# Feed-forward operands computed beside the second half of a mixer's out product, in pools of their own

## The chip, the cores and the metric

One core of a Trainium2 chip runs the whole program. The metric is the device time of one execution in microseconds (us), the median of several runs.

## The reference, cut to what matters

Two blocks on 512 tokens of 1024 features, in float32. The first (attention, neighbourhood attention, pooling, a long convolution, experts) isn't touched. The second puts 16 meta tokens ahead and runs two layers, each a mixer and then a SwiGLU:

```python
def _swiglu(h, w_gu, w_down):
    gate, up = jnp.split(h @ w_gu, 2, axis=-1)
    return (jax.nn.silu(gate) * up) @ w_down
...
    for layer in range(DEPTH_2):
        j = layer // 2
        if layer % 2 == 0:
            h = h + _mixer_rglru_swa(_rmsnorm(h, mix_norm_ab[j]), ...)
        else:
            h = h + _mixer_retention(_rmsnorm(h, mix_norm_ret[j]), ...)
        h = h + _swiglu(_rmsnorm(h, ffn_norm[layer]), ffn_w_gu[layer], ffn_w_down[layer])
```

Both mixers end in a product with an out matrix that is added to `h`: `concatenate([y_rnn, y_att]) @ w_out` and `(silu(g) * o) @ w_out`.

## The kernel before, in words

The residual `hT` holds the features on the partitions in 8 tiles f of 128 and the 528 tokens along a row. Every float32 product is three matmuls: `split` (L296, L299) makes a high part by a cast (ACT) and a low part by a subtraction (DVE), of weights and of activations, and PE adds high·high, high·low and low·high. Weights come over SP's DMA queue into a ring of three raw tiles with three split pairs `whi`, `wlo`.

**Mixer 0** (`mixer_ab`): RG-LRU and sliding-window attention write their outputs, split, to `abm0` and `abm1`. The out product (L2460 to L2464) runs over two halves o of the mix, and in each over eight rows f in the order `FORDER` = 0, 4, 1, 5, 2, 6, 3, 7: load and split one 128x512 weight tile, 24 matmuls (L1798: two token halves, four slices, three parts), and two adds to `hT` (L2464, DVE). **Mixer 1** (`mixer_ret`) does the same for two halves hh of its heads from `ry0`, `ry1`: 24 matmuls of 512 columns a row, one add (L2595).

**Feed-forward** (`swiglu`). The gate and up products use a Strassen-like scheme over four row pairs (f, f+4). For a row, ACT writes `hid0` = gain·hT (L2143), squares hT (L2145, L2148) and POOL sums the squares (L2149). When both rows of a pair are there, `operands` (L1826) makes seven parts of them: two subtractions on POOL (L1835, L1839), two on DVE (L1837, L1840), and splits of 264, 528 and 1056 columns into `xo0` and `xo1` (L296 on ACT, L299 on DVE). The four-part sums lie in a tile `s24` (pairs 0 and 2) or `rawF` (pairs 1 and 3). Both tiles also serve the weights: `rawF` is the fourth raw tile, `s24` holds sums of weight tiles.

A job is one of 22 row blocks of w_gu. Its weights are a plain tile (L1866, SP), a tile of sums, which is a plain load (L1871, SP) and then a second load that adds onto it from POOL's queue (L1876), and a half tile `a22` (L1981). ACT casts them (L1900, L1918, L1926, L1988), DVE or POOL makes the low parts (L1890, L1991), and PE runs four products A, Bb, C, D (L1852). Within the first job PE also does the sum for the norm (L2157), ACT and DVE make the scale R (L2158, L2159), and ACT copies a product for the gate (L2085, L2088, L2099). The down jobs follow each group (L2062, adds L2072). Weight pairs rotate over five slots: the ring's three, then F0, F1 of the feed-forward's pool.

What orders the work: each engine runs its instructions in order. PE's order is written by hand; those of ACT, DVE and POOL are set by a scheduler up to the first job and by hand from the second. Memory of a closed pool is handed on: the first write into a tile waits for the last use of what lay there. `swiglu` opened one pool after the mixer's pools had closed, with `hid0`, `xo0`, `xo1`, `rawF`, `s24` and the rest in it.

Of the kernel before, what the change touches and what calls it, by code (L numbers as in the profile page):

```python
# [2117 lines left out]

def swiglu(B, layer, cuts):
    b, nc, tc = B.b, B.nc, B.tc  # L2120
    V, S_, G, T_ = nc.vector, nc.scalar, nc.gpsimd, nc.tensor
    A = b.A
    o0, W = cuts[0][0], cuts[0][1] - cuts[0][0]
    gain = b.smv("ffng", 8 * layer, 8)
    with ExitStack() as es:
        pool = es.enter_context(tc.tile_pool(name=f"ffn{layer}", bufs=1, reuse_waits="tile"))
        es.enter_context(tc.manual_schedule(engines={mybir.EngineType.PE}))
        xo = [b.t(pool, [P, 4, 7 * W], F32R, tag="xo0")]
        b.t(pool, [P, 1056], tag="s24")
        b.t(pool, [P, 8, 2 * W], tag="hid1")  # L2130
        for i in range(FSLOTS):
            for n in ("whi", "wlo"):
                b.t(pool, [P, 1024], F32R, tag=f"{n}F{i}")
        b.t(pool, [P, 1, W], tag="p1")
        xo.append(b.t(pool, [P, 4, 7 * W], F32R, tag="xo1"))
        wn = Wino(B, pool, W, cuts, [(B.ring, "")] * 3 + [(pool, f"F{i}") for i in range(FSLOTS)],
                  [(B.ring, "raw")] * 3 + [(pool, "rawF")], b.hT)
        xg = b.t(pool, [P, 8, 2 * W], tag="hid0")
        R, a = b.t(B.xp, [P, 2 * W], tag="xR"), B.tmp(1)[:, :2 * W]
# [293 lines left out]

def mixer_ab(B, dbg):
    b, nc, tc = B.b, B.nc, B.tc
    A = b.A
    lin = B.cyc(0, 1, 2, 3, 6, 7)
    with ExitStack() as es:
# [20 lines left out]
        for o in range(2):
            for i, f in enumerate(FORDER):  # L2460
                acc = abo[0] if o == 0 and i < 4 else abo[1]
                w = load_split(b, B.ring, A["ab_out"][f, :, 512 * o:512 * o + 512], 512)
                for a, (a0, a1) in zip(B.lin(w, [m[:, 4 * o:4 * o + 4] for m in mix], HV, 4, acc=acc), HV):
                    nc.vector.tensor_tensor(b.hT[:, f, a0:a1], b.hT[:, f, a0:a1], a[:, :a1 - a0], op=ALU.add)  # L2464

# [3 lines left out]

def mixer_ret(B, dbg):  # L2470
    b, nc, tc = B.b, B.nc, B.tc
# [3 lines left out]
    with ExitStack() as es:  # L2475
        B.xx = es.enter_context(tc.tile_pool(name="xret", bufs=1, reuse_waits="tile"))
        pool = es.enter_context(tc.tile_pool(name="ret", bufs=1, reuse_waits="tile"))
        for i in range(2):
            b.t(pool, [P, 8, 512], tag=f"ry{i}")
# [121 lines left out]
def block2(b, out, dbg):  # L2601
    nc, tc = b.nc, b.tc
    with tc.tile_pool(name="hres", bufs=1, reuse_waits="tile") as hp, \
# [6 lines left out]

        def dump(n):
            if dbg is not None and n in dbg:
                nc.sync.dma_start(dbg[n].rearrange("(f p) n -> p f n", p=P), b.hT)
        mixer_ab(B, dbg)
        dump("h_ab")
        swiglu(B, 0, HV)
        dump("h_f0")
        mixer_ret(B, dbg)
        dump("h_ret")
        swiglu(B, 1, ((16, 272), (272, 528)))  # L2620
# [40 lines left out]
```

## Time and profile before

| | |
|---|---|
| median of 3 runs (lowest, highest) | 2386.99 us (2381.87, 2392.85) |
| the profiled execution: its own time | 2384.32 us |
| its span, mean granted TensorE clock | 2382.5 us, 0.957 |
| PE busy | 2204.3 us, 93% of the span |
| DVE, ACT, POOL busy | 1544.1, 1108.2, 823.9 us |

Times in views are microseconds from the start of the span. The 1.8 us between the span and the execution's own time lie outside the profile. An engine's idle time stands in brackets behind the instruction that ended it, with what released it.

### The profile page before, as it was taken

How to read it: one execution, taken by the hardware profiler on the slowest of the kernel's cores; microseconds unless marked ns; L12 is line 12 of the kernel's file. 1: busy time of each engine (PE TensorE's matmuls, PEld its weight loads, DVE VectorE, ACT ScalarE, POOL GpSimd, SP SyncE). 2: the span in 40 equal slices, each digit the busy share in tenths (PEclk: the TensorE clock that was granted, in tenths of full speed). 3: DMA queues.
4: the chain of work that ended last, by engine and by line, in shares of the span. 5: the costliest groups of instructions: out<-in, count | busy, mean ns of one | idle time of the engine just before them, and what ended most of it. 6: DMA issues, size and time to landing. Idle time of an engine off the chain costs nothing.

```text
span 2382.5 us, 34349 instructions
## 1 busy us (share of the span) xinstructions
PE 2204.3 (93%) x13248; PEld 1882.8 (79%) x13248; DVE 1544.1 (65%) x2138; ACT 1108.2 (47%) x1697; POOL 823.9 (35%) x543
## 2 busy tenths in 40 slices
PE   7799989978999888899699999999999997999999
PEld 1577768757777667767699999978788875999999
DVE  5764886557885776765687685665544555776854
ACT  4324654326876764545454353433323344543532
POOL 2325122225774644430344251322201213442512
PEclk9999989988999999979899999999999998899999
DMA  7563121577988752100365464422222222664652
GB/s 252 188 216 126 37 96 35 215 259 245 344 304 317 264 197 79 56 18 14 97 164 169 120 180 111 110 77 75 68 90 77 80 71 73 175 173 124 178 124 85
DMA packets 112289, 338.58 MB, mean 142 GB/s; under 512 B 14280, under 2 KB 17624, under 8 KB 112118
## 3 DMA queue, kind: packets, MB, share of 16 engines
q1 hardware_dynamic: 91168, 288.85, 35.6%
q0 software_dynamic: 11536, 31.75, 7.0%
q10 hardware_dynamic: 9414, 15.72, 2.0%
q8 instruction: 106, 1.74, 0.3%
q14 instruction: 65, 0.53, 0.1%
HBM read 325.65 MB, written 19.47 MB: 145 GB/s over the span
## 4 chain that ended last, share of the span: by engine, by line
PE 54%; DVE 4%; ACT 1%; issue 1%; POOL 1%; DMA 1%; DVEq 0%; POOLq 0%; ACTq 0%
PE p L1852 18%; PE p L1798 13%; PE p L2062 11%; PE p L2535 4%; PE p L2569 1%; PE p L2399 1%; DMA rawF<-in_gu 1%; PE p L1787 1%; PE p L2425 1%; PE p L2566 1%; PE p L2538 1%; DVE xo L299 0%; PE gu L1637 0%; PE p L2227 0%; PE p L2422 0%
## 5 line engine op out<-in xcount | busy, mean ns | idle before, releaser
L296 ACT CAST whi<-raw 128x1024 fp32r<-128x1024 f32 (+1 forms) x237 | 239.8, 1022 | 298.5 <-PE p L1798 132.6
L299 DVE TENSOR_TENSOR wlo<-raw,whi 128x1024 fp32r<-128x1024 f32 (+1 forms) x178 | 253.4, 1442 | 90.9 <-ACT whi L296 87.3
L1852 PE MATMUL p<-xo,whi 128*128 128x264 f32 (+1 forms) x1312 | 251.7, 291 | 42.4 <-DVE xo L299 15.1
L1852 PEld LDWEIGHTS p<-xo,whi 128*128 128x128 f32 x1312 | 209.2, 194 | 47.0 <-DVE xo L299 17.3
L1798 PE MATMUL p<-x,whi 128*128 128x264 f32 (+1 forms) x992 | 224.7, 330 | 4.4 <-DVE xt L2291 2.1
L299 POOL TENSOR_TENSOR wlo<-raw,whi 128x1024 fp32r<-128x1024 f32 x59 | 153.7, 2613 | 198.2 <-ACT whi L296 179.2
L1852 PE MATMUL p<-xo,wlo 128*128 128x264 f32 (+1 forms) x656 | 189.1, 288 | 3.3 <-DVE wlo L1890 3.3
L1798 PEld LDWEIGHTS p<-x,whi 128*128 128x128 f32 x992 | 157.7, 188 | 27.5 <-issue 5.2
L1852 PE MATMUL p<-xo,whiF 128*128 128x264 f32 (+1 forms) x800 | 149.1, 285 | 0.0
L1798 PE MATMUL p<-x,wlo 128*128 128x264 f32 (+1 forms) x496 | 141.2, 332 | 0.9 <-POOL wlo L299 0.9
L1852 PEld LDWEIGHTS p<-xo,wlo 128*128 128x128 f32 x656 | 127.4, 194 | 3.9 <-DVE wlo L1890 3.9
L1852 PEld LDWEIGHTS p<-xo,whiF 128*128 128x128 f32 x800 | 125.5, 191 | 0.0
L2062 PE MATMUL p<-hid,whi 128*128 128x264 f32 (+1 forms) x768 | 123.4, 282 | 0.0
L1360 PE MATMUL gu<-wlo,xh 128*128 128x512 f32 x272 | 110.6, 406 | 11.4 <-DVE wlo L299 6.2
L2072 DVE TENSOR_TENSOR hT<-hT,p 128x264 f32<-128x264 f32 (+1 forms) x96 | 36.5, 421 | 129.2 <-PE p L2062 129.2
L1852 PE MATMUL p<-xo,wloF 128*128 128x264 f32 (+1 forms) x400 | 114.3, 286 | 0.0
L1359 PE MATMUL gu<-whi,xh 128*128 128x512 f32 x272 | 112.3, 413 | 0.0
L1361 PE MATMUL gu<-whi,xlo 128*128 128x512 f32 x272 | 109.6, 403 | 1.6 <-DVE xlo L299 1.6
L2062 PEld LDWEIGHTS p<-hid,whi 128*128 128x128 f32 x768 | 105.1, 188 | 0.0
L2062 PE MATMUL p<-hid,whiF 128*128 128x264 f32 (+1 forms) x640 | 103.6, 284 | 0.0
L1890 DVE TENSOR_TENSOR wlo<-raw,whi 128x1024 fp32r<-128x1024 f32 (+1 forms) x60 | 91.6, 1530 | 2.7 <-ACT whi L1900 1.7
L1798 PEld LDWEIGHTS p<-x,wlo 128*128 128x128 f32 x496 | 83.9, 188 | 10.8 <-issue 1.6
(1314 smaller groups left out, 6064.2 us busy)
## 6 DMA issues: line engine op xcount, KB each, us to landing
raw<-in_moe SPq DMA_DIRECT2D x115, 512.0 KB, 5.2
raw<-in_gu SPq DMA_DIRECT2D x66, 512.0 KB, 4.7
sp<-in_moe SPq DMA_DIRECT2D x48, 512.0 KB, 8.3
mixAB<-in_ada SPq DMA_DIRECT2D x32, 512.0 KB, 4.4
raw<-in_down SPq DMA_DIRECT2D x24, 512.0 KB, 3.6
a<-in_gu SPq DMA_DIRECT2D x44, 256.0 KB, 2.6
raw<-in_gu POOLq DMA_DIRECT2D x22, 512.0 KB, 5.7
rawF<-in_gu SPq DMA_DIRECT2D x22, 512.0 KB, 4.4
```

The costliest lines, as they stand in the source:

```text
L296: i = nc.scalar.copy(hi, src)
L299: self.last = i, (lo_eng or nc.vector).tensor_tensor(lo, src, hi.bitcast(F32), op=ALU.subtract)
L1359: T_.matmul(acc, xh[:, k], hi[:, w], start=k == 0, stop=False)
L1360: T_.matmul(acc, xh[:, k], lo[:, w], start=False, stop=False)
L1361: T_.matmul(acc, xl[:, k], hi[:, w], start=False, stop=k == 7)
L1787: self.nc.tensor.matmul(a[:, :c1 - c0], w[wi][:, ks], x[xi][:, k, c0:c1], start=k == 0 and wi == 0 and xi == 0, stop=k == nk - 1 and wi == 1)
L1798: nc.tensor.matmul(a[:, :c1 - c0], w[wi][:, ks], x[xi][:, k, c0 - o:c1 - o], start=k == 0 and wi == 0 and xi == 0, stop=k == nk - 1 and wi ...
L1852: T_.matmul(bank[:, :W], w[wi][:, 512 * i + 128 * k:512 * i + 128 * k + 128], xo[xi][:, k, W * j:W * j + W], start=first and k == 0 and wi ...
L1890: lo = lambda w, src, n=1024: V.tensor_tensor(w[1][:, :n], src, w[0][:, :n].bitcast(F32), op=ALU.subtract)
L2062: nc.tensor.matmul(a_[:, :W], w[wi][:, ks], put.hid[xi][:, k, W * j:W * j + W], start=k == 0 and wi == 0 and xi == 0, stop=k == nk - 1 and ...
L2072: V.tensor_tensor(self.hT[:, f, c0:c1], self.hT[:, f, c0:c1], a_[:, :W], op=ALU.add)
L2535: T_.matmul(acc[t], x[xi][:, kk, ts_], w[wi][:, ws], start=kk == 0 and xi == 0 and wi == 0, stop=kk == 7 and xi == 1)
```

## The change

`swiglu` becomes a class `Swiglu` with `early`, which opens pools and computes the operands, and `run`, the rest. Each mixer keeps its product's operands (`abm`, `ry`) in a pool of their own and closes everything else ahead of the second half of its out product. There `early` opens two pools, one with `hid0`, `s24`, `rawF` and the slot F0, one with `xo0`, `xo1`. `run` opens the rest (`hid1`, the slot F1, `a22` and small tiles) once the mixer has closed. The slots now rotate as F0, F1, then the ring's three. Code that wrote out `hT` for tests, unused here, is gone. Lines move by some 6 to 35: `hid0` is L2150 after, the squares L2152 and L2155, the sums L2156, `operands` L1832 to L1842, the loads L1872, L1877, L1882, the casts L1906, L1924, L1932, L1994, the products L1858, R L2177, L2178, the copies L2091, L2094, L2105, the adds of the out products L2488 and L2630.

```diff
@@ class Wino
-        self.slots, self.raws, self.nraws = itertools.cycle(slots), itertools.cycle(raws), len(raws)
+        self.slots_, self.raws, self.nraws = slots, itertools.cycle(raws), len(raws)
+        self.early_pool = pool
...
-        tt = b.t(self.pool, [P, 1056], tag=("s24", "rawF")[f % 2])[:, :4 * W].rearrange("p (a n) -> p a n", a=4)
+        tt = b.t(self.early_pool, [P, 1056], tag=("s24", "rawF")[f % 2])[:, :4 * W].rearrange("p (a n) -> p a n", a=4)
...
+    def late_pool(self, pool):
+        self.pool = pool
+        self.slots = itertools.cycle([(pool, k) if k == "F1" else (p, k) for p, k in self.slots_])
@@ swiglu
+class Swiglu:
...
+    def early(self):
...
+        pg = self.pg = es.enter_context(tc.tile_pool(name=f"ffng{n}", bufs=1, side="right", reuse_waits="tile"))
+        po = es.enter_context(tc.tile_pool(name=f"ffno{n}", bufs=1, side="right", reuse_waits="tile"))
+        xg = b.t(pg, [P, 8, 2 * W], tag="hid0")
+        wn = self.wn = Wino(B, pg, W, self.cuts, [(pg, "F0"), (pg, "F1")] + [(B.ring, "")] * 3,
+                            [(B.ring, "raw")] * 3 + [(pg, "rawF")], b.hT)
+        xo = self.xo = [b.t(po, [P, 4, 7 * W], F32R, tag=f"xo{i}") for i in range(2)]
...
+    def run(self):
...
+        pool = es.enter_context(tc.tile_pool(name=f"ffn{layer}", bufs=1, reuse_waits="tile"))
+        es.enter_context(tc.manual_schedule(engines={mybir.EngineType.PE}))
+        wn.late_pool(pool)
...
@@ mixer_ab
+        work = ExitStack()
+        pm = es.enter_context(tc.tile_pool(name="abmix", bufs=1, reuse_waits="tile"))
...
+        for i, f in enumerate(FORDER):
+            out(0, i, f)
+        work.close()
+        for i, f in enumerate(FORDER):
+            out(1, i, f)
+        for _ in nxt.early():
+            pass
@@ mixer_ret
+            if hh:
+                work.close()
             for f in FORDER:
                 w = load_split(b, B.ring, A["ret_out"][8 * hh + f])
                 a = B.lin(w, (yh, yl), LV, o=16)[0]
                 V.tensor_tensor(b.hT[:, f, 16:], b.hT[:, f, 16:], a, op=ALU.add)
+        for _ in nxt.early():
+            pass
```

What the engines' orders make of it, at three places. ACT, end of mixer 0, before: the last casts of out weights (`whi` 128x512) have only squares (`xt`) between them; all `hid` and `xo` come behind.

```order
L296 CAST whi_11712<-raw_11711 128x512
L2148 ACTIVATE xt_2583_11802<-hT_9255 128x528
L1900 CAST whi_11855<-raw_11839 128x1024
L2148 ACTIVATE xt_2585_11810<-hT_9255 128x528
L2148 ACTIVATE xt_2586_11821<-hT_9255 128x528
L2143 ACTIVATE hid_2575_11762<-hT_9255,sm_59 128x528 x2
L296 CAST xo_2566_11753<-hid_2575_11762 128x264
L296 CAST xo_2566_11753<-hid_2575_11762 128x528
```

After: operands of earlier pairs stand ahead of the last out weight's cast, and a cast of a summed weight tile (L1932) stands ahead of `hid` of the last pair.

```order
L296 CAST whi_11720<-raw_11719 128x512
L1906 CAST whiF_2594_11860<-raw_11844 128x1024
L2150 ACTIVATE hid_2568_11759<-hT_9255,sm_59 128x528
L2155 ACTIVATE xt_2577_11800<-hT_9255 128x528
L296 CAST xo_2569_11760<-hid_2568_11759 128x264
L2150 ACTIVATE hid_2568_11759<-hT_9255,sm_59 128x528
L2155 ACTIVATE xt_2579_11808<-hT_9255 128x528
L296 CAST xo_2569_11760<-hid_2568_11759 128x528
L1932 CAST whi_11879<-raw_11846 128x1024
L1906 CAST whi_11886<-raw_11848 128x1024
L2150 ACTIVATE hid_2568_11759<-hT_9255,sm_59 128x528
L296 CAST xo_2569_11760<-s_2578_11805 128x1056
```

`hid` and `xo` moved up by as many rows as three of the four pairs need; L1932 now stands between the third pair's and the last pair's work. SP, the same place, before (raw tiles of the ring, halves `a22`, and the fourth raw tile `rawF`):

```order
L1866 DMA raw_2589_11839<-in_gu 128x1024
L1871 DMA raw_2590_11841<-in_gu 128x2x512
L1866 DMA raw_2591_11843<-in_gu 128x1024
L1981 DMA a22_2593_11847<-in_gu 128x512
L1981 DMA a22_2596_11851<-in_gu 128x512
L1981 DMA a22_2643_12086<-in_gu 128x512
L1871 DMA rawF_2592_11845<-in_gu 128x2x512
L1866 DMA raw_2604_11870<-in_gu 128x1024
```

After:

```order
L1872 DMA raw_2584_11844<-in_gu 128x1024
L1877 DMA raw_2585_11846<-in_gu 128x2x512
L1872 DMA raw_2586_11848<-in_gu 128x1024
L1987 DMA a22_2588_11852<-in_gu 128x512
L1987 DMA a22_2591_11856<-in_gu 128x512
L1872 DMA raw_2599_11875<-in_gu 128x1024
L1877 DMA raw_2602_11883<-in_gu 128x2x512
L1987 DMA a22_2638_12091<-in_gu 128x512
L1877 DMA rawF_2587_11850<-in_gu 128x2x512
L1987 DMA a22_2660_12224<-in_gu 128x512
```

`rawF`'s first load now stands behind two more raw tiles of the ring. ACT, end of mixer 1, before (`whi` 128x1024 with L296 are out weights):

```order
L296 CAST whi_19332<-raw_19331 128x1024
L2148 ACTIVATE xt_3698_19419<-hT_9255 128x512
L1900 CAST whi_19472<-raw_19456 128x1024
L2148 ACTIVATE xt_3700_19427<-hT_9255 128x512
L2148 ACTIVATE xt_3701_19438<-hT_9255 128x512
L2143 ACTIVATE hid_3690_19379<-hT_9255,sm_59 128x512 x2
L296 CAST xo_3681_19370<-hid_3690_19379 128x256
```

After:

```order
L296 CAST whi_19344<-raw_19343 128x1024
L2150 ACTIVATE hid_3676_19381<-hT_9255,sm_59 128x512
L2155 ACTIVATE xt_3685_19422<-hT_9255 128x512
L296 CAST xo_3677_19382<-hid_3676_19381 128x256
L1932 CAST whi_19501<-raw_19468 128x1024
L2150 ACTIVATE hid_3676_19381<-hT_9255,sm_59 128x512
L2155 ACTIVATE xt_3687_19430<-hT_9255 128x512
L296 CAST xo_3677_19382<-hid_3676_19381 128x512
```

Here too the summed tile's cast L1932 stands ahead of the last row's `hid`.

## Rows read from the trace of the kernel before

**Rows 1.** The page, the chain that ended last, by engine.
```profile
PE 54%; DVE 4%; ACT 1%; issue 1%; POOL 1%; DMA 1%; DVEq 0%; POOLq 0%; ACTq 0%
```

**Rows 2.** Stretches: us; PE, PEld, DVE, ACT, POOL busy; PEclk, DMA share, GB/s.
```profile
1141.00:1165.40 24.40, 24.37 (x200) 24.16 (x198) 11.09 (x24) 10.79 (x18) 9.32 (x8) 1.00 0.56 152
1165.40:1208.30 42.90, 19.19 (x89) 16.71 (x90) 33.13 (x36) 21.87 (x33) 15.36 (x14) 0.64 0.36 98
1208.30:1250.00 41.70, 41.70 (x344) 41.70 (x344) 38.10 (x46) 24.68 (x39) 22.50 (x16) 1.00 0.65 166
1976.00:2003.50 27.50, 27.50 (x123) 22.61 (x121) 8.34 (x9) 9.76 (x14) 10.76 (x9) 1.00 0.35 96
2003.50:2044.20 40.70, 18.69 (x89) 16.33 (x89) 31.52 (x36) 20.30 (x30) 12.83 (x11) 0.62 0.39 104
```

**Rows 3.** Waits of PE, 1160 to 1215 us: total us, times, longest.
```profile
PE p L1852 <- DVE xo L299: 8.1, 4, 2.7
PE p L1852 <- ACT whi L1926: 5.7, 1, 5.7
```

**Rows 4.** Timeline of ACT, 1143 to 1212 us: start us, us, instruction, idle before.
```profile
1157.35 0.65 ACT L2148 ACTIVATE xt<-hT 128x528 f32<-128x528 f32 x1 [0.36 <-DVE hT L2464]
...
1163.22 0.65 ACT L2148 ACTIVATE xt<-hT 128x528 f32<-128x528 f32 x1 [2.29 <-DVE hT L2464]
1163.77 1.35 ACT L2143 ACTIVATE hid<-hT,sm 128x528 f32<-128x528 f32 x2
...
1176.37 1.36 ACT L2143 ACTIVATE hid<-hT,sm 128x528 f32<-128x528 f32 x2
...
1197.77 1.05 ACT L1926 CAST whi<-rawF 128x1024 fp32r<-128x1024 f32 x1 [4.48 <-DMA rawF<-in_gu]
...
1202.55 0.38 ACT L2099 COPY u<-p 128x264 f32<-128x264 f32 x1
```

**Rows 5.** Timeline of DVE, 1143 to 1215 us.
```profile
1157.17 0.68 DVE L299 TENSOR_TENSOR wlo<-raw,whi 128x512 fp32r<-128x512 f32 x1
...
1165.29 0.77 DVE L2464 TENSOR_TENSOR hT<-hT,p 128x264 f32<-128x264 f32 x2 [2.17 <-PE p L1798]
1166.09 0.96 DVE L1837 SCALAR_TENSOR_TENSOR s<-s,hid 128x264 f32<-128x264 f32 x1
...
1167.86 0.42 DVE L1840 SCALAR_TENSOR_TENSOR s<-s,hid 128x264 f32<-128x264 f32 x1
...
1182.84 1.26 DVE L299 TENSOR_TENSOR xo<-rawF,xo 128x1056 fp32r<-128x1056 f32 x1
```

**Rows 6.** Timeline of POOL, 1143 to 1215 us.
```profile
1159.40 0.98 POOL L1876 DMA_DIRECT2D raw<-in_gu  x1
...
1166.01 0.74 POOL L1839 TENSOR_TENSOR s<-hid 128x264 f32<-128x264 f32 x1
...
1191.27 0.90 POOL L1876 DMA_DIRECT2D rawF<-in_gu  x1 [4.37 <-DMA rawF<-in_gu]
```

**Rows 7.** Timeline of SP's DMA issues, 1150 to 1215 us.
```profile
1185.62 0.43 SPq L1871 DMA_DIRECT2D rawF<-in_gu  x1
```

**Rows 8.** Timeline of PE: the second job's product Bb starts, layer 0 and layer 1.
```profile
1208.24 0.41 PE L1852 MATMUL p<-xo,whi 128*128 128x264 f32 x2
...
2044.18 0.44 PE L1852 MATMUL p<-xo,whi 128*128 128x256 f32 x2
```

**Rows 9.** Timeline of DVE, 2000 to 2030 us.
```profile
2003.51 0.69 DVE L2595 TENSOR_TENSOR hT<-hT,p 128x512 f32<-128x512 f32 x1 [4.75 <-PE p L1798]
...
2019.39 1.23 DVE L299 TENSOR_TENSOR xo<-rawF,xo 128x1024 fp32r<-128x1024 f32 x1
```

**Rows 10.** Timeline of ACT, 1546 to 1562 us (the retention mixer's norm).
```profile
1548.78 4.48 ACT L1704 ACTIVATE x<-hT,sm 128x528 fp32r<-128x528 f32 x7
```

**Rows 11.** Timeline of PE, 1546 to 1556 us (feed-forward ends, retention begins).
```profile
1551.65 0.94 PE L1798 MATMUL p<-x,whi 128*128 128x512 f32 x4
```

**Rows 12.** Timeline of DVE, 900 to 921 us (the second block's first norm).
```profile
909.64 8.95 DVE L1734 SCALAR_TENSOR_TENSOR x<-xl,f_gn,x 128x512 fp32r<-128x512 f32 x7
```

More of the change, by code (lines that the diff above doesn't have):

```diff
@@ L2116, with __init__ @@
 PARTS = 8, 8, 6
[L2119 to L2139, printed above, removed]
+class Swiglu:
+    def __init__(self, B, layer, cuts):
+        self.B, self.layer, self.cuts, self.es = B, layer, cuts, ExitStack()
+    def early(self):
+        B, tc, es = self.B, self.B.tc, self.es
+        b = B.b
+        S_, G = b.nc.scalar, b.nc.gpsimd
+        o0, W = self.cuts[0][0], self.cuts[0][1] - self.cuts[0][0]
+        gain = b.smv("ffng", 8 * self.layer, 8)
+        n = self.layer
+        pg = self.pg = es.enter_context(tc.tile_pool(name=f"ffng{n}", bufs=1, side="right", reuse_waits="tile"))
[4 more added lines that the diff above has]
+        xo = self.xo = [b.t(po, [P, 4, 7 * W], F32R, tag=f"xo{i}") for i in range(2)]
+        a = self.a = B.tmp(1)[:, :2 * W]
         gens = {}
@@ L2180, in put @@
             if f == 0:
-                put.hid = [b.t(pool, [P, 8, 2 * W], F32R, tag=f"hid{k}") for k in range(2)]
+                put.hid = [b.t(k, [P, 8, 2 * W], F32R, tag=t_) for k, t_ in ((self.pg, "hid0"), (pool, "hid1"))]
             S_.copy(put.hid[0][:, f], uf)
@@ L2192, in swiglu @@
             k0 += nk
-        wn.run(jobs, 5, xo, put, norm, last)
+        wn.run(jobs, 5, self.xo, put, norm, last)
+        es.close()
 FORDER = 0, 4, 1, 5, 2, 6, 3, 7
@@ L2431, with mixer_ab @@
 LRU_AT = (1, 3, 5, 7)
[L2434 removed]
+def mixer_ab(B, nxt):
     b, nc, tc = B.b, B.nc, B.tc
@@ L2438, in mixer_ab @@
     with ExitStack() as es:
-        B.xx = es.enter_context(tc.tile_pool(name="xab", bufs=1, reuse_waits="tile"))
+        work = ExitStack()
+        pm = es.enter_context(tc.tile_pool(name="abmix", bufs=1, reuse_waits="tile"))
+        b.t(pm, [P, 8, NT], F32R, tag="abm0")
+        b.t(pm, [P, 8, NT], F32R, tag="abm1")
+        B.xx = work.enter_context(tc.tile_pool(name="xab", bufs=1, reuse_waits="tile"))
         with tc.manual_schedule(engines={mybir.EngineType.PE}):
@@ L2445, in mixer_ab @@
                 x, R = B.first(b.xl2, lambda k: B.lin_step(k, ws, B.x, pre))
-        pool = es.enter_context(tc.tile_pool(name="ab", bufs=1, reuse_waits="tile"))
-        mix = [b.t(pool, [P, 8, NT], F32R, tag=f"abm{i}") for i in range(2)]
+        mix = [b.t(pm, [P, 8, NT], F32R, tag=f"abm{i}") for i in range(2)]
+        pool = work.enter_context(tc.tile_pool(name="ab", bufs=1, reuse_waits="tile"))
         lg = lru(B, pool, x, R, *mix, B.cyc(0, 1, 2, 3), B.cyc(6, 7))
@@ L2455, in mixer_ab, with out, mixer_ret @@
         b.x2c.close()
-        att = es.enter_context(tc.tile_pool(name="swa", bufs=1, reuse_waits="tile"))
+        att = work.enter_context(tc.tile_pool(name="swa", bufs=1, reuse_waits="tile"))
         swa(B, att, qkv, *mix, B.cyc(3, 4, 5), B.cyc(6), B.cyc(7))
         abo = B.cyc(0, 1, 2), B.cyc(0, 1, 2, 3, 4, 5)
[L2459 to L2464, printed above, removed]
+        def out(o, i, f):
+            acc = abo[0] if o == 0 and i < 4 else abo[1]
+            w = load_split(b, B.ring, A["ab_out"][f, :, 512 * o:512 * o + 512], 512)
+            for a, (a0, a1) in zip(B.lin(w, [m[:, 4 * o:4 * o + 4] for m in mix], HV, 4, acc=acc), HV):
+                nc.vector.tensor_tensor(b.hT[:, f, a0:a1], b.hT[:, f, a0:a1], a[:, :a1 - a0], op=ALU.add)
+        for i, f in enumerate(FORDER):
[5 more added lines that the diff above has]
+            pass
 LV = ((16, 528),)
-def mixer_ret(B, dbg):
+def mixer_ret(B, nxt):
     b, nc, tc = B.b, B.nc, B.tc
@@ L2475, in mixer_ret @@
     with ExitStack() as es:
[L2476 to L2477 removed]
+        work = ExitStack()
+        py = es.enter_context(tc.tile_pool(name="rety", bufs=1, reuse_waits="tile"))
         for i in range(2):
[L2479 removed]
+            b.t(py, [P, 8, 512], F32R, tag=f"ry{i}")
+        B.xx = work.enter_context(tc.tile_pool(name="xret", bufs=1, reuse_waits="tile"))
+        pool = work.enter_context(tc.tile_pool(name="ret", bufs=1, reuse_waits="tile"))
         x, R0 = B.norm(sm("mnret"), HV)
@@ L2498, in mixer_ret @@
         for hh in range(2):
-            yh, yl = [b.t(pool, [P, 8, 512], F32R, tag=f"ry{i}") for i in range(2)]
+            yh, yl = [b.t(py, [P, 8, 512], F32R, tag=f"ry{i}") for i in range(2)]
             for h2 in range(2):
@@ L2609, in block2 @@
         B = Blk2(b, ring, xp, ps)
[L2611 to L2620, printed above, removed]
+        ffn = [Swiglu(B, n, cuts) for n, cuts in enumerate((HV, ((16, 272), (272, 528))))]
+        mixer_ab(B, ffn[0])
+        ffn[0].run()
+        mixer_ret(B, ffn[1])
+        ffn[1].run()
         for f in range(8):
```

9 lines of the change are left out of this document (8 added, 1 removed).

## The prediction

> **What bounds the kernel now.** The chain that ended last runs through PE for 54% of the span, no other engine is named with over 4% [rows 1]: time is won where PE stands still. So I looked for long gaps of PE that the change touches, stretch by stretch [rows 2]. In the second half of mixer 0's out product (1141 to 1165.4) PE is busy throughout, 200 matmuls in 24.37 us, 0.122 each, at granted clock 1.00. In the 42.9 us behind it, up to the second job's product Bb at 1208.24 [rows 8], it runs 89 matmuls. They take 0.216 us each at a mean clock of 0.64, which between the levels 1.2 and 2.4 GHz means mostly the lower one. From there on it is busy 41.70 of 41.70 us at 1.00. Layer 1 has the same hole: 89 matmuls in 40.7 us (2003.5 to 2044.2). At 0.122 the two lots would need 11 us each, so the holes hold at most 42.9 - 10.9 + 40.7 - 10.9 = 62 us.
>
> What PE waits for there, first and longest, is `xo` (8.1 us in four waits on its low part), and 5.7 us for a weight cast L1926 [rows 3]. On ACT `hid` begins at 1163.77, as the out product ends, and the last pair's `hid` only at 1176.37 [rows 4]. DVE ends the last low part of `xo`, read from `rawF`, at 1182.84 + 1.26 = 1184.10 [rows 5]. Only then is `rawF` free for weights: SP issues its load 1.52 us later, at 1185.62 [rows 7]. POOL issues the load that adds to it at 1191.27 [rows 6], ACT can cast at 1197.77 [rows 4]. So the load chain of `rawF` takes 1197.77 - 1185.62 = 12.15 us and starts from the end of the operands. ACT stands at that cast, and the copy `u` that PE needs next comes behind it, at 1202.55 [rows 4].
>
> **The change, part by part.** The number and size of the instructions stay; the gain is the operands' time beside the out product.
>
> *Do they fit beside it?* A row of the out product takes (1163.22 - 1157.35) / 2 = 2.94 us [rows 4], a pair 5.87. ACT's own work in the second half is 10.79 us, DVE's 11.09, in 200 / 24 = 8.3 rows [rows 2], so 2.6 and 2.7 a pair. A pair of operands adds to ACT two `hid` (1.35) and casts of 264 + 528 + 1056 columns, 1.9 us at 1.05 per 1024 [rows 4], together 5.85. To DVE it adds the same columns at 1.26 per 1056, 2.2 us, and two subtractions of 0.42 [rows 5], together 5.7. Both are just under 5.87. DVE gets longer where POOL runs: its subtraction took 0.96 at 1166.09, when POOL's of 1166.01 (0.74) ran [rows 5, 6], and 0.42 when none did. I let half of POOL's four operations a pair cost 0.54: 1.1 us, so DVE falls behind by some 0.9 us a pair, 2.8 after three. An out weight's low part (0.68 [rows 5]) then comes about that much later; the order of ACT puts the last out weight's cast a full row ahead of its use, so I price PE's loss in the out product at nothing, with 2.8 us as the bad end.
>
> *Layer 0.* ACT's cast of the summed raw tile now stands ahead of the last pair's `hid`. Its second load was issued at 1159.40 [rows 6]; with 6.5 us to land (1191.27 to 1197.77, the other such load) it is there at 1165.9, just as the last out row is added (1165.29 + 0.77 [rows 5]). Two casts of 1.05 bring the last pair's `hid` to 1168. It needs, as before, 1184.10 - 1176.37 = 7.7 us to its last low part: 1175.7, and with half of DVE's lag 1177.0, 7.1 us earlier than before. SP moves two raw loads ahead of `rawF`; they wait for ring tiles cast earlier, and `rawF` stays the last to become free. Then 1.52 + 12.15 + 1.05 for the cast, and 1.1 for its low part: Bb at 1192.8 rather than 1208.24. This is **-15.4 us**, more than the operands' 7.1, because the cast of `rawF` now stands behind the copy `u`, R and the other weights on ACT; PE's first job no longer waits for it, and 89 matmuls at 0.216, 19.2 us from 1165.4, are over by 1184.6 and their waits. Ends: -6.6 (rival two) and -18.
>
> *Layer 1.* A row takes 24 x 27.5 / 123 = 5.4 us and DVE is busy 8.34 of 27.5, ACT 9.76 [rows 2]: the operands fit easily. The last row is added at 2003.51 + 0.69; only its own half of the last pair is left. I take 7 us, a bit under the 7.7 of a whole pair: 2011.2 rather than 2019.39 + 1.23 = 2020.6 [rows 9]. The same 15.8 us behind it put Bb at 2027.0, not 2044.18 [rows 8]: **-17.2 us**. Ends: -10.1 and -22.
>
> *Handed-on memory.* The retention mixer's `x` now lies where the feed-forward's `hid` was, and the last down jobs use the ring. Its first write, at 1548.78 before [rows 10], must wait for the last down matmul, just ahead of 1551.65, where PE took up `x` [rows 11]. PE starts at least 0.65 later, at most the 2.9 us of that shift; I take **+1.5** for it, weights that come later included. The second block's first norm meets the same at its start; DVE's low parts of 8.95 / 7 = 1.28 us [rows 12] pace it either way: **+0.5**, ends 0 and 1.28. The slots' new order and the rest cost nothing: from the second job on PE is busy all the time, with ACT at 24.68 and DVE at 38.10 of 41.70 [rows 2].
>
> Sum: -15.4 - 17.2 + 1.5 + 0.5 = -30.6. The profiled execution took 2384.3 (2.7 under the median of the runs), so 2353.7; I say **2353**.
>
> **Rivals.** *One: DVE and POOL lock each other.* The Trainium skill says ("SBUF — State Buffer", section "Who interferes with whom") that a VectorE instruction with two SBUF inputs and a GpSimd instruction that reads SBUF exclude each other, the later one waiting for the whole of the earlier. The trace agrees for the pair of 0.96 and 0.74 above. If every POOL operation met such an instruction, POOL's time would add in full to DVE's. POOL is busy 9.32 us there already [rows 2], and eight subtractions of 0.74 make it 15.2; DVE would have 4 x 5.7 + 15.2 = 38 us to do from 1141.9 (eight rows of 2.94 ahead of 1165.4) and end at 1180, with out weights up to 10 us late. Layer 0 would then win about nothing: -17.2 + 2 gives 2369. Against it: from 1141 to 1165.4 POOL was busy 9.32 us and DVE's 24 instructions still took 0.46 us on average [rows 2], so most of POOL's work there met nothing that grew.
> *Two: the seam only moves.* If from the end of the operands to Bb the old 24.1 us (1184.10 to 1208.24) and 23.6 us (2020.6 to 2044.18) remain, because PE's first job at the lower clock and not `rawF` ends last, the gain is the operands' 7.1 + 9.4 alone: -14.5 with the memory, 2370. For it: the lower clock will come in this hole too.
> *Three: it does not do what it says,* and some `hid` or `xo` still waits for the mix tiles. Then 2384 + 2, 2386. Against: ACT's new order.
> *Four, slower: PE stalls a little in every row of the second halves and the clock falls.* Its place is the weight's low part on DVE, its price the 0.122 that becomes 0.216 or more. Rows at half speed cost 8 x 2.94 = 23.5 and 8 x 5.4 = 43 us, and the first job's 19 us still follow: Bb at 1165.4 + 23.5 + 19.2 = 1208.1 and 2003.5 + 43 + 19 = 2065.5, together +21.3 and with the memory 2408. It decides once DVE needs more than a row's time in layer 1; 8.34 of 27.5 us speaks against.
>
> **How the numbers follow.** My forecast, between 2341 (both seams at the good ends, -40, with 3 for the spread of runs) and 2364, has 0.64; rivals one and two 0.14 and 0.13; three 0.05; four 0.04. The range 2341 to 2372 holds the forecast and the first two, less their tails. No change means within 0.5%, 12 us, about what a measurement of this kernel can tell. Faster: the forecast, and rivals one and two (0.6 to 0.7% each) but for 0.03: 0.88. Same: 0.03 + 0.05. Slower: 0.04.
>
> **What would show it.** Right: `hid` on ACT from the first rows of the second halves on; last `xo` from `rawF` near 1177 and 2011; SP's `rawF` load 1.5 us behind; PE at 1.00 through the second halves; about 27 us from the last mix matmul to the second job's Bb, where 42.9 and 40.7 stood. Wrong: low parts of out weights among PE's waits (one, four); PE's wait behind the operands ended by something other than `rawF`'s weights (two); the retention mixer starting over 3 us late.

## The result and the profile after

The changed kernel takes **2359.83 us**, the median of 7 runs (2350.06 to 2373.58), against 2386.09 for the kernel before in 7 runs (2381.87 to 2392.85). The ratio is 0.989, 95% interval 0.9863 to 0.9917: 26 us or 1.1% faster. The forecast was 2353, range 2341 to 2372. The profiled execution is the fastest of the seven, 2350.06 us, with a span of 2348.3. It must not be compared as a whole: 6.7 us of its lead were there before the second block began, in code that is the same (the last transposes end at 900.03, before at 906.71). So everything below is read between two points of one profile.

The page of the change, busy times and the chain by engine [rows 1]:

```profile
PE 2192.0 (93%) x13248; PEld 1875.2 (80%) x13248; DVE 1555.2 (66%) x2138; ACT 1107.3 (47%) x1697; POOL 823.8 (35%) x543
...
PE 53%; DVE 3%; ACT 2%; DMA 1%; POOL 1%; issue 1%; DVEq 0%; POOLq 0%; ACTq 0%; SPq 0%
```

PE still bounds the kernel. Stretches of the change (us, PE, PEld, DVE, ACT, POOL busy, granted clock, DMA share, GB/s) for the last eight rows of mixer 0's out product, the hole behind it up to Bb of the second job, the time behind that, and the hole of layer 1:

```profile
1130.20:1153.80 23.60, 23.19 (x190) 22.98 (x188) 20.15 (x31) 15.74 (x26) 11.06 (x10) 1.00 0.36 97
1153.80:1187.20 33.40, 16.30 (x90) 14.62 (x88) 24.26 (x24) 14.82 (x23) 15.65 (x12) 0.69 0.49 129
1187.20:1229.00 41.80, 41.05 (x324) 40.84 (x325) 38.20 (x47) 24.78 (x38) 19.92 (x15) 0.96 0.71 176
1986.20:2008.80 22.60, 13.05 (x88) 12.04 (x87) 13.19 (x13) 10.30 (x17) 9.36 (x9) 0.85 0.60 157
```

Against [rows 2]: DVE is busy 20.15 of 23.6 us beside the out product, where it was 11.09 of 24.4, and PE still runs 190 matmuls at 1.00 there. The first hole is 33.4 us instead of 42.9, the second 22.6 instead of 40.7. The clock in the first is 0.69 after 0.64: still mostly the lower level.

The last mix matmul and the first of Bb in layer 0, on PE [rows 8]:

```profile
1153.42 0.40 PE L1798 MATMUL p<-abm,wlo 128*128 128x264 f32 x2
...
1187.18 0.51 PE L1858 MATMUL p<-xo,whiF 128*128 128x264 f32 x2 [3.64 <-ACT whiF L1932]
```

Bb now waits for `rawF`'s cast. PE's waits from 1125 to 1205 us (total, times, longest) [rows 3]:

```profile
PE p L1858 <- ACT xo L296: 8.3, 2, 4.8
PE p L1858 <- DVE xo L299: 3.9, 2, 3.2
PE p L1858 <- ACT whiF L1932: 3.6, 1, 3.6
...
PE p L1798 <- DVE wlo L299: 0.4, 1, 0.4
```

The four waits for low parts of `xo` (8.1 us) are two (3.9), the wait for the cast of a raw tile (5.7) is gone, but 8.3 us for high parts (4.0 before) and 3.6 us for `rawF`'s cast stand there now. Why the operands still end late stands in DVE's timeline, 1138 to 1200 us [rows 5]:

```profile
1142.59 0.76 DVE L2488 TENSOR_TENSOR hT<-hT,p 128x264 f32<-128x264 f32 x2
1143.32 1.82 DVE L299 TENSOR_TENSOR wlo<-raw,whi 128x512 fp32r<-128x512 f32 x1
...
1145.98 1.55 DVE L1838 SCALAR_TENSOR_TENSOR rawF<-rawF,hid 128x264 f32<-128x264 f32 x1
...
1156.10 1.80 DVE L299 TENSOR_TENSOR xo<-hid,xo 128x528 fp32r<-128x528 f32 x1
...
1158.51 0.42 DVE L1841 SCALAR_TENSOR_TENSOR s<-s,hid 128x264 f32<-128x264 f32 x1
...
1161.68 0.76 DVE L2488 TENSOR_TENSOR hT<-hT,p 128x264 f32<-128x264 f32 x2
...
1171.30 1.26 DVE L299 TENSOR_TENSOR xo<-rawF,xo 128x1056 fp32r<-128x1056 f32 x1 [0.59 <-ACT xo L296]
```

and in POOL's beside it [rows 6]:

```profile
1142.01 1.28 POOL L1836 TENSOR_TENSOR rawF<-hid 128x264 f32<-128x264 f32 x1 [2.71 <-ACT hid L2150]
1143.25 1.34 POOL L2156 TENSOR_TENSOR xt<-xt,xt 128x528 f32<-128x528 f32 x1
...
1145.72 1.51 POOL L2156 TENSOR_TENSOR xt<-xt,xt 128x528 f32<-128x528 f32 x1
...
1155.84 1.49 POOL L2156 TENSOR_TENSOR xt<-xt,xt 128x528 f32<-128x528 f32 x1
...
1178.61 0.85 POOL L1882 DMA_DIRECT2D rawF<-in_gu  x1 [2.29 <-DMA rawF<-in_gu]
```

The low part of an out weight took 0.68 us before and takes 1.82 here, in the worst case. It starts at 1143.32 under POOL's sum, which runs to 1144.59, and ends 0.55 later. The subtraction at 1145.98 ends 0.30 behind POOL's sum of 1145.72, the low part at 1156.10 0.57 behind that of 1155.84. The adds of 1142.59, which read one operand from PSUM, ran under POOL's subtraction of 1142.01 and weren't longer (0.76 for two). From 1137.11 to the last add ten such instructions took 8.2 us more than the shortest of their form. **The last add comes at 1161.68, 7.9 us behind the last mix matmul**, and the last low part ends at 1171.30 + 1.26 = 1172.56, 18.7 us behind it, exactly as far as before (1184.10 - 1165.37 [rows 5]).

ACT [rows 4] and SP [rows 7] show where the hole shrank all the same:

```profile
1162.47 0.74 ACT L2150 ACTIVATE hid<-hT,sm 128x528 f32<-128x528 f32 x1 [1.31 <-DVE hT L2488]
...
1178.31 0.38 ACT L2105 COPY u<-p 128x264 f32<-128x264 f32 x1 [4.47 <-PE p L1858]
...
1186.08 1.04 ACT L1932 CAST whiF<-rawF 128x1024 fp32r<-128x1024 f32 x1 [4.29 <-DMA rawF<-in_gu]
```

```profile
1172.59 0.38 SPq L1877 DMA_DIRECT2D rawF<-in_gu  x1
```

The copy `u` now comes at 1178.31, ahead of `rawF`'s cast at 1186.08; before it stood behind it. SP issues the load of `rawF` as the operands end, 0.03 us behind, where 1.52 us lay between. Whether that is owed to the early operands is asked of `none_early` below.

Layer 1, DVE's last add and last low part [rows 9], and Bb on PE [rows 8]:

```profile
1987.42 0.68 DVE L2630 TENSOR_TENSOR hT<-hT,p 128x512 f32<-128x512 f32 x1
...
1993.55 3.62 DVE L299 TENSOR_TENSOR xo<-rawF,xo 128x1024 fp32r<-128x1024 f32 x1 [2.42 <-ACT xo L296]
```

```profile
2008.81 0.51 PE L1858 MATMUL p<-xo,whiF 128*128 128x256 f32 x2 [1.85 <-ACT whiF L1932]
```

The operands end at 1993.55 + 3.62 = 1997.17, 11.0 us behind the last mix matmul (1986.20), where 17.1 stood; the last low part is one more that stood behind POOL, whose two low parts of half tiles (L1997) took 2.79 us from 1993.30 on. The retention mixer's first matmul [rows 11] comes 0.6 us behind the last down matmul (1533.29), with which it was level; ACT's first writes of its `x`, which began 2.9 us ahead of it before [rows 10], now wait for PE's last down matmuls:

```profile
1533.08 1.36 ACT L1704 ACTIVATE x<-hT,sm 128x528 fp32r<-128x528 f32 x2 [2.73 <-PE p L2068]
```

```profile
1533.87 1.34 PE L1798 MATMUL p<-x,whi 128*128 128x512 f32 x3 [0.58 <-ACT x L1704]
```

### The profile page after: what moved, and what is told of

Read it like the earlier page. It is cut to its first block, busy times and chain, and to the rows that moved or that the text cites. A ratio compares the mean times of both kernels' runs of the same rounds, so it can differ in the third digit from the quotient of the medians.

```text
span 2348.3 us, 34349 instructions
## 1 busy us (share of the span) xinstructions
PE 2192.0 (93%) x13248; PEld 1875.2 (80%) x13248; DVE 1555.2 (66%) x2138; ACT 1107.3 (47%) x1697; POOL 823.8 (35%) x543
## 4 chain that ended last, share of the span: by engine, by line
PE 53%; DVE 3%; ACT 2%; DMA 1%; POOL 1%; issue 1%; DVEq 0%; POOLq 0%; ACTq 0%; SPq 0%
PE p L1858 18%; PE p L1798 13%; PE p L2068 11%; PE p L2568 4%; PE p L2602 1%; DMA rawF<-in_gu 1%; PE p L2419 1%; PE p L2445 1%; PE p L2599 1%; PE p L2571 1%; DVE xo L299 0%; POOL xt L1741 0%; DVE wlo L299 0%; PE p L2442 0%; PE gu L1637 0%
## 5 line engine op out<-in xcount | busy, mean ns | idle before, releaser
L296 ACT CAST whi<-raw 128x1024 fp32r<-128x1024 f32 (+1 forms) x237 | 239.8, 1021 | 280.9 <-PE p L1798 121.6
L1858 PE MATMUL p<-xo,whi 128*128 128x264 f32 (+1 forms) x1216 | 224.7, 284 | 11.8 <-ACT xo L296 8.0
L1858 PEld LDWEIGHTS p<-xo,whi 128*128 128x128 f32 x1216 | 189.1, 190 | 12.9 <-ACT xo L296 8.5
L1858 PE MATMUL p<-xo,whiF 128*128 128x264 f32 (+1 forms) x896 | 171.1, 289 | 13.6 <-ACT whiF L1932 5.5
L1858 PE MATMUL p<-xo,wlo 128*128 128x264 f32 (+1 forms) x608 | 172.5, 284 | 0.0
L1858 PEld LDWEIGHTS p<-xo,whiF 128*128 128x128 f32 x896 | 143.0, 195 | 14.9 <-ACT whiF L1932 5.9
L2068 PE MATMUL p<-hid,whi 128*128 128x264 f32 (+1 forms) x928 | 149.7, 283 | 0.0
L1858 PE MATMUL p<-xo,wloF 128*128 128x264 f32 (+1 forms) x448 | 129.7, 290 | 3.5 <-DVE wloF L1896 3.5
L2068 PEld LDWEIGHTS p<-hid,whi 128*128 128x128 f32 x928 | 126.7, 188 | 0.2
L1858 PEld LDWEIGHTS p<-xo,wlo 128*128 128x128 f32 x608 | 115.5, 190 | 0.0
L2068 PE MATMUL p<-hid,wlo 128*128 128x264 f32 (+1 forms) x464 | 93.2, 282 | 0.0
```

The costliest lines, as they stand in the source:

```text
L296: i = nc.scalar.copy(hi, src)
L1858: T_.matmul(bank[:, :W], w[wi][:, 512 * i + 128 * k:512 * i + 128 * k + 128], xo[xi][:, k, W * j:W * j + W], start=first and k == 0 and wi ...
L2068: nc.tensor.matmul(a_[:, :W], w[wi][:, ks], put.hid[xi][:, k, W * j:W * j + W], start=k == 0 and wi == 0 and xi == 0, stop=k == nk - 1 and ...
```

## The experiments

In each profile I take four stretches: **mixer 0**, from the end of the last transposes of the first block to the last mix matmul; **layer 0**, on to the last down matmul; **mixer 1**, on to its last mix matmul; **layer 1**, on to the end of the last add. The expectations were written before each run; the numbers in us, the ratio with its interval:

| kernel | median | ratio to before | mixer 0 | layer 0 | mixer 1 | layer 1 |
|---|---|---|---|---|---|---|
| before | 2386.09 | | 258.7 | 386.5 | 451.7 | 375.7 |
| before_2 | 2383.7, one run | | 259.3 | 386.4 | 451.7 | 376.0 |
| the change | 2359.83 | 0.989 (0.9863 to 0.9917) | 253.8 | 379.5 | 452.9 | 358.8 |
| none_early | 2377.95 | 0.9971 (0.9953 to 0.9988) | 253.2 | 386.2 | 451.8 | 375.3 |
| ab_only | 2375.14 | 0.9955 (0.9939 to 0.9971) | 253.9 | 379.3 | 453.1 | 375.5 |
| ret_only | 2367.76 | 0.9932 (0.9905 to 0.9958) | 257.0 | 386.3 | 451.8 | 362.1 |
| adds_first | 2359.5 | 0.9885 (0.9863 to 0.9907) | 257.7 | 378.6 | 453.0 | 361.3 |
| no_pool | 2358.42 | 0.9887 (0.9868 to 0.9905) | 258.8 | 380.9 | 453.1 | 358.6 |
| tt3 | 2351.15 | 0.9853 (0.983 to 0.9875) | 252.2 | 374.2 | 452.6 | 359.1 |
| tt3_sub | 2343.29 | 0.9832 (0.9812 to 0.9853) | 253.3 | 372.0 | 452.6 | 357.5 |
| tt3_sum | 2343.89 | 0.9825 (0.9805 to 0.9844) | 255.9 | 370.9 | 452.5 | 357.8 |
| tt3_nopool | 2343.17 | 0.9821 (0.9799 to 0.9843) | 251.5 | 370.8 | 452.7 | 356.6 |

**One layer, or none, early.** `ab_only` (late = layer 1), `ret_only` (layer 0) and `none_early` (both) keep the split pools and the slots' order, and compute a late layer's operands behind the mixer, in pools on the other side, where `abm` or `ry` lay (LATE stands for the late layers):

```diff
-        pg = self.pg = es.enter_context(tc.tile_pool(name=f"ffng{n}", bufs=1, side="right", reuse_waits="tile"))
+        pg = self.pg = es.enter_context(tc.tile_pool(name=f"ffng{n}", bufs=1, side="left" if n in LATE else "right", reuse_waits="tile"))
...
     def run(self):
+        if self.layer in LATE:
+            for _ in self.early():
+                pass
...
-        for _ in nxt.early():
+        for _ in nxt.early() if nxt.layer not in LATE else ():
             pass
```

The pool of `xo` is treated alike. `ab_only`:

> Layer 0's operands stay early; layer 1's are computed behind mixer 1 again, in pools that lie where its product's operands lay. Theory (seam by seam): in the profile of the change the stretch from the last mix matmul to the second job's Bb shrank from 42.8 to 33.4 us, of which 2.4 is given back in the job behind, so seam 1 is worth about -7 and the retention mixer's start costs +1.4: -5.6 us, 2380 against 2386. Rival (what lies ahead of seam 1, 6 us at the second block's start and in mixer 0, also comes from the change, through the place of x in memory): -12 or more.

It came to 2375.14, 10.7 us under before by the ratio (6.9 to 14.6). The theory's 5.6 lies outside, the rival's 12 inside. The stretches settle layer 0: 379.3 and 379.5 with the operands early, here and in the change, 386.3 without, so **-7.0** against before (386.5). The rest comes from mixer 0, as the rival has it. `ret_only`:

> Layer 1's operands stay early; layer 0's are computed behind mixer 0 again. Theory: seam 2 is worth -15, the retention mixer's start +1.4: -14 us, 2372. Rival (part of the gain comes from ahead of seam 1): -20. From the last mix matmul of layer 0 to Bb I expect some 41 to 43 us again, and in layer 1 about 21 to 22.

2367.76, 16 us under before (10 to 23), which tells the two apart no better. Bb comes 38.2 and 24.0 us behind the last mix matmuls, not at 41 to 43 and 21 to 22. Layer 1 is 362.1 us here, 358.8 in the change and 375.7 before: **-14 to -17**. `none_early`:

> The pools stay split and the slots rotate as in the change, but both layers' operands are computed behind the mixers, in pools that lie where the out products' operands lay. Theory: the second block's start -0.9 (the same in five profiles of the new layout), the retention mixer's start +1.3, both holes as before (about 42 and 40 us from the last mix matmul to Bb): 2385 to 2387. Rival (the layout itself wins some 5 us in mixer 0): 2381.

2377.95, 2.9 to 11 us under before: nearer to the rival. Mixer 0 is 5.4 us shorter here. Layer 0, mixer 1 and layer 1 are as long as before within 0.4 us, but in the two layers that is a balance and not a zero. Both holes shrank, with nothing computed early: Bb comes 38.0 and 33.6 us behind the last mix matmuls (42.9 and 40.7 before; about 42 and 40 expected), though in layer 0 the operands end later, at 23.1 us (18.7 before, 18.7 in the change). From their end to Bb it is 14.9 us, where the change has 14.6 (24.1 before). On ACT, `u` now comes straight behind `rawF`'s cast, ahead of R; then Bb on PE:

```profile
1193.07 1.05 ACT L1932 CAST whiF<-rawF 128x1024 fp32r<-128x1024 f32 x1 [4.31 <-DMA rawF<-in_gu]
1194.03 0.37 ACT L2105 COPY u<-p 128x264 f32<-128x264 f32 x1
```

```profile
1197.49 0.41 PE L1858 MATMUL p<-xo,whiF 128*128 128x264 f32 x2
```

By the 300th matmul behind the last mix matmul 2.4 us of the lead over before are left in layer 0 and 4.4 in layer 1. Behind it PE is busy all the time, and slower than before. The same 260 us of layer 1 in before, in none_early and in the change:

```profile
2080.00:2340.00 260.00, 260.00 (x2199) 260.00 (x2198) 183.63 (x234) 113.85 (x169) 99.31 (x66) 1.00 0.56 150
```

```profile
2080.00:2340.00 260.00, 260.00 (x2170) 260.00 (x2168) 182.75 (x231) 110.91 (x164) 97.58 (x64) 1.00 0.54 146
```

```profile
2080.00:2340.00 260.00, 260.00 (x2208) 259.90 (x2207) 169.02 (x225) 101.28 (x149) 87.30 (x57) 1.00 0.49 136
```

From the 300th to the 2500th matmul one takes 118.4, 120.0 and 117.7 ns in layer 1 and 121.7, 122.7 and 121.8 in layer 0, at a granted clock of 1.00 each time; every profile with a late layer has the slow pace in that layer. What sets it isn't shown; the late layers' pools lie elsewhere. So, counted up to the 300th matmul, the new slots and pools win 2.4 us in layer 0 and 4.4 in layer 1, and the operands' early start 4.7 and 10.7 more, as far as the late layers' place does not matter there. The middle seam's price (mixer 1 at 453 rather than 451.7, **+1.2**) appears only where layer 0 is early.

**Was mixer 0's lead chance?** `before_2` is the kernel before, unchanged:

> The kernel before, once more, for a second profile of it. In nine profiles of the new layout the sliding-window part of mixer 0 (from 122 to 144 us behind the second block's first product) is 3.9 us shorter than in the one profile of before, at a higher granted clock (0.76 against 0.66 in that stretch), with the same instructions. Layout theory (PE starts some 1 us sooner there, and the clock rises sooner): 148.9 us again, and 257 or so to the last mix matmul. Rival (chance of that one execution): 144, and 252 to 254.

Counted, as there, from the start of the second block's first matmul, the attention's part came at 145.0, nearer to the rival's 144 than to 148.9, but the last mix matmul at 258.4 rather than 252 to 254. Each hypothesis has one half. The same 25 us of that part in before, in before_2 and in none_early (columns as above):

```profile
1027.80:1052.80 25.00, 22.08 (x65) 13.71 (x65) 14.61 (x32) 10.77 (x20) 12.59 (x14) 0.69 0.07 22
```

```profile
1026.40:1051.40 25.00, 23.39 (x75) 15.16 (x76) 17.31 (x42) 11.87 (x25) 12.60 (x14) 0.70 0.07 22
```

```profile
1027.60:1052.60 25.00, 23.02 (x79) 15.20 (x80) 18.57 (x45) 12.37 (x27) 12.59 (x14) 0.76 0.07 22
```

The granted clock is 0.69, 0.70 and 0.76. Ten profiles of the new layout have mixer 0 at 251.5 to 258.8 us, 254.7 on average, two of the old at 258.7 and 259.3. Some 4 us of the gain thus seem to lie in code that the change moved only in memory, though three of the ten (257.0 to 258.8) are as long as the old ones, or nearly. The second block's first product has no clear part in it: it ends 22.3 us behind the last transposes in all ten, and 23.21 and 21.70 us behind them in the two of the old. What sets the rest stays open.

**Does DVE have too much to do, or does it stand behind POOL?** `no_pool`:

```diff
-        G.tensor_tensor(tt[:, 0], b11, b12, op=ALU.subtract)
+        V.tensor_tensor(tt[:, 0], b11, b12, op=ALU.subtract)
...
-        G.tensor_tensor(tt[:, 2], b22, b12, op=ALU.subtract)
+        V.tensor_tensor(tt[:, 2], b22, b12, op=ALU.subtract)
...
-                G.tensor_tensor(a, a, s, op=ALU.add)
+                b.nc.vector.tensor_tensor(a, a, s, op=ALU.add)
```

> The two subtractions of an operand pair and the sums of squares move from POOL to DVE, for both layers; 15 instructions a layer, 8 x 0.34 + 7 x 0.6 = 6.9 us more work for DVE. Lock theory: DVE's instructions with two tiles as inputs stood behind POOL's for some 9 us in layer 0's second half; that goes, so DVE ends the last out add within 4 us of the last mix matmul (8 in the profile of the change), no subtraction on DVE is over 0.5 us there, and seam 1 wins 3 to 6 us: 2354 to 2357. Load theory (DVE simply has too much to do): the last add comes 10 us or more behind the last mix matmul and the time is 2360 or more.

DVE's timeline, a subtraction, the out rows' last add and two low parts of `xo`, the last one too:

```profile
1144.76 0.43 DVE L1838 SCALAR_TENSOR_TENSOR s<-s,hid 128x264 f32<-128x264 f32 x1 [0.21 <-ACT hid L2150]
...
1160.80 0.77 DVE L2488 TENSOR_TENSOR hT<-hT,p 128x264 f32<-128x264 f32 x2
...
1170.42 1.76 DVE L299 TENSOR_TENSOR xo<-hid,xo 128x528 fp32r<-128x528 f32 x1
...
1174.53 1.25 DVE L299 TENSOR_TENSOR xo<-rawF,xo 128x1056 fp32r<-128x1056 f32 x1
```

With more work DVE is *in time*: the last add starts at 1160.80, as the last mix matmul ends (1160.88), and the operands end 14.9 us behind it, not 18.7. Up to the last add no such instruction is stretched. Behind it two are, to 1.49 and 1.76 us (0.43 and 0.70 elsewhere), and there POOL runs its two low parts of half tiles (L1997, 2.68 us from 1168.93). The load theory falls. But layer 0 is 380.9, 1.4 longer than in the change, and the time is the same. PE's wait from 1135 to 1215 us has a new name:

```profile
PE p L1858 <- DVE wloF L1896: 16.8, 2, 12.9
```

The scheduler had moved DVE's low part of the first weight behind all operands; PE stood 12.9 us for it with A hardly begun, and had nearly all of that product still to do when the operands came. That order also took weight work from in front of the last add, so not all of the 7.9 us is POOL's: the next run tells the two apart.

**Weights behind the adds.** `adds_first`:

```diff
+        with B.tc.issue_after(self.added):
             for i in range(ahead):
                 more()
                 for _ in range(4):
                     self.tick()
```

(`added` is the out product's last add; the block holds DVE's work on the first weights.)

> On DVE all of the feed-forward's weight work (low parts and sums of the first weight tiles) is put behind the last add of the out product, for both layers. Order theory: three low parts, 1.77 + 2.91 us in the profile of the change, stood ahead of the last two rows' adds; without them the last add of layer 0 comes 4 us sooner, seam 1 wins 2 to 4 us: 2356 to 2358. Rival: the low parts are needed so early by the first job that PE waits for them in place of xo, and nothing is won: 2360.

The last add came 5.2 us behind the last mix matmul (1168.40 - 1163.23), 2.7 sooner than in the change and not 4, and layer 0 is 0.9 shorter; in time nothing. Here, as in no_pool, no weight work of the feed-forward stands ahead of the last add, and the add is still 5.2 us late with POOL's work on POOL, and not late with it on DVE. The rival's waits are there:

```profile
PE p L1858 <- DVE wloF L1896: 9.3, 2, 8.9
PE p L1858 <- ACT whiF L1932: 4.7, 1, 4.7
PE p L1858 <- DVE wlo L1896: 4.4, 1, 4.4
```

**Is the load chain of `rawF` the end of the hole?** `tt3` puts the last pair's sums into the place of the second `hid` tile, which is free until the first job is done. The last two rows f of `early` then run once the late pool is open:

```diff
-        tt = b.t(self.early_pool, [P, 1056], tag=("s24", "rawF")[f % 2])...
+        if f == 3:
+            tt = self.tt3
+        else:
+            tt = b.t(self.early_pool, [P, 1056], tag=("s24", "rawF")[f % 2])...
...
-        for _ in nxt.early():
-            pass
+        nxt.rest = nxt.early()
+        for _ in range(6):
+            next(nxt.rest)
...
         wn.late_pool(pool)
+        wn.tt3 = b.t(pool, [P, 8, 2 * W], tag="hid1")...
+        for _ in self.rest:
+            pass
```

> The last odd pair's sums lie in the place of the feed-forward's second hid tile, which is written later, and no longer in rawF; so rawF's load may go once pair 1 is split, some 20 us sooner. Chain theory (the load chain of rawF behind the end of the operands ends the hole): Bb in layer 0 about 29 us behind the last mix matmul, where the change has 33.4, in layer 1 about 20 where it has 22.6, no wait of PE for a cast of rawF: 2351 to 2354. Rival (PE's first job at the lower clock ends last anyway): no change, 2359 to 2360.

2351.15. SP issues the load 22.6 us ahead of the operands' end (1183.41), the cast no longer waits for a DMA, and no wait of PE from 1130 to 1210 us is for `rawF`:

```profile
1160.82 0.37 SPq L1880 DMA_DIRECT2D rawF<-in_gu  x1
```

```profile
1186.72 1.05 ACT L1935 CAST whiF<-rawF 128x1024 fp32r<-128x1024 f32 x1 [0.91 <-PE p L1861]
```

```profile
PE p L1861 <- ACT xo L296: 9.5, 2, 4.8
PE p L1861 <- DVE xo L299: 3.3, 2, 1.7
PE p L1861 <- DVE wloF L1899: 1.3, 1, 1.3
```

Bb comes at 30.6 us in layer 0 (29 expected, 33.4 in the change). Layer 0 is 374.2 us, 5.3 less than in the change, with operands that end 19.3 us behind the last mix matmul, later than its 18.7. So the chain, and not the operands' end alone, ended the hole. Layer 1 didn't gain (359.1 against 358.8; Bb at 26.2 us, where 20 were expected): half a miss.

**The lock, with the chain out of the way.** `tt3_sub` adds the first two edits of no_pool, `tt3_sum` its third, `tt3_nopool` all three:

> As tt3, and the subtractions of an operand pair move from POOL to DVE. Lock theory with the chain out of the way: DVE's lag behind the out product shrinks from 8 to 5 us or less, the operands end some 2 to 3 us sooner and now Bb with them: 2348 to 2351. Rival (DVE has too much work): the lag grows by 8 x 0.34 = 2.7 us and so does Bb: 2355.

> As tt3, and the sums of squares move from POOL to DVE. Lock theory: DVE gets 7 x 0.6 = 4.3 us more work and loses about half of the 9 us that it stood behind POOL: its lag stays or shrinks by up to 2 us; 2349 to 2353. Rival (too much work): lag and Bb grow by 4 us: 2356.

> As tt3, with both the subtractions and the sums of squares on DVE. Lock theory: nothing of POOL is left that reads beside DVE, the operands of layer 0 end some 14 us behind the last mix matmul (19.3 in tt3, 17.4 and 15.1 with one of the two moved) and the third scaling by R (the second job's) 35 to 36 us behind it (40.4, 39.0, 37.2): 2340 to 2343. Rival: DVE's first low part of weights now comes behind all operands, PE waits for it (12.9 us in no_pool), and layer 0 falls back to 40: 2346 to 2349.

2343.29, 2343.89 and 2343.17. Layer 0 falls from 374.2 to 372.0, 370.9 and 370.8, and the operands end 17.4, 15.1 and 14.5 us behind the last mix matmul instead of 19.3: less waiting behind POOL is worth more than the work that DVE takes over. The lag of the last add goes from 6.2 us in tt3 to 6.4, 2.7 and none: moving the subtractions alone did not shrink it to 5 or less, as expected. In layer 1, where DVE has room, the add comes later with each move (2.1 us behind the last mix matmul in tt3, 4.0 in tt3_nopool), and the operands still end sooner (12.2 us, not 15.3). The medians fell by more (7 to 8 us) than the two layers (3.8 to 5.9), and the first two came out below all that was expected of them; the rest isn't located. In `tt3_nopool` the last add and the last low part:

```profile
1157.84 0.77 DVE L2494 TENSOR_TENSOR hT<-hT,p 128x264 f32<-128x264 f32 x2
...
1171.13 1.25 DVE L299 TENSOR_TENSOR xo<-hid,xo 128x1056 fp32r<-128x1056 f32 x1
```

(The last mix matmul ends at 1157.92.) The rival's wait came too:

```profile
PE p L1861 <- DVE wloF L1899: 12.5, 1, 12.5
```

It cost nothing, since PE's other waits there (14.1 us in three kinds in tt3) went to 1.4; the second job's scaling came at 36.9 us, a little later than expected. In time, both moves together win nothing measurable over either alone. All three beat both kernels: 1.7 to 1.8% under before, where the change has 1.1%.

## Why the prediction was right, and where not

The time lay in the range and the sign was right; the gain is 26 us where 31 were forecast. That it came so near is in part luck: layer 0 fell short by 8.4 us, and mixer 0 gave some 4 that nobody forecast.

- **Where the kernel is bound, and that PE loses nothing in the out product:** right. 190 matmuls in 23.19 us, one wait of 0.4 us.
- **Layer 1, -17.2:** measured -17.0 in the profile of the change, -13.6 in ret_only. Its steps were off against each other: the operands end 11.0 us behind the last mix matmul rather than 7.7, and from there to Bb it is 11.6 us rather than 15.8. Of the 17.0 some 1.9 come from quicker matmuls behind the 300th and 4.4 from the new slots and pools, by none_early; the forecast had neither.
- **Middle seam, +1.5:** +1.2.
- **The second block's start, +0.5:** not to be told from two profiles of before: -0.9 against the one, +0.6 against the other. Mixer 0 as a whole is some 4 us shorter, which nobody forecast; this hides part of the next error.
- **Layer 0, -15.4:** -7.0 (9.5 at Bb, of which 2.5 are given back in the next job, where PE, after its waits, begins at the lower clock: 0.22 us a matmul from 1187 to 1191, at a granted clock of 0.61). The step that failed is "I let half of POOL's four operations a pair cost 0.54: 1.1 us, so DVE falls behind by some 0.9 us a pair, 2.8 after three". Ten instructions cost 8.2 us, up to 1.14 each: here a POOL operation could cost DVE nearly all of its own time, and not 0.54. That was the price of a short POOL operation (0.74 us); the sums of squares take 1.3 to 1.5, and the trace of before had one of them beside a DVE instruction that takes 0.43 alone in no_pool (the lines are below). The sum also left out the low parts of the first feed-forward weights ahead of the last adds: three of them (1.77 and 2.91 us), where one of 1.23 stood before. So the lag was 7.9 us, not 2.8, and the operands' end won nothing on the last mix matmul against before.

```profile
1179.53 1.48 POOL L2149 TENSOR_TENSOR xt<-xt,xt 128x528 f32<-128x528 f32 x1
```

```profile
1179.78 1.52 DVE L299 TENSOR_TENSOR xo<-hid,xo 128x264 fp32r<-128x264 f32 x1
```

- **What carried layer 0 instead** is the step behind it: from the operands' end to Bb 14.6 us (24.1 before; 15.8 forecast). The forecast's reason, `rawF`'s cast behind `u` and R on ACT, isn't needed for it: in none_early the cast stands ahead of both, the operands come late, and it is 14.9 us. The shorter step goes with the new slots and pools, of which the prediction said that they "cost nothing"; against that kernel the early operands put Bb 4.6 us sooner (33.4, not 38.0).
- **Rival one** had the right mechanism. The Trainium skill has it as a rule ("SBUF — State Buffer", section "Who interferes with whom"): of a VectorE instruction with two SBUF inputs and a GpSimd instruction that reads SBUF, the later waits for the whole of the earlier. The traces agree, with the ends 0.30 to 0.57 us behind POOL's and the adds from PSUM unhurt. Its price, nothing won in layer 0 and weights up to 10 us late, was too high, since PE waited 0.4 us in the out product and the step behind the operands paid in any case. **Rival two** failed: the 24.1 us became 14.6, and the 23.6 became 11.6. (Its ends of -6.6 and -10.1 in the two layers' sums don't agree with the 7.1 and 9.4 it is given later; their totals nearly do.) **Rivals three and four** didn't come: `hid` moved, and the clock stayed at 1.00 beside the out product.
